# Feed-forward products of a decoder trunk: from wide and narrow matmuls in turn to runs of one width

## Chip, core and metric

The kernel runs on one core of a Trainium2 chip. The metric is the device time of one execution in microseconds (us). The time before is the median of three runs.

## What is computed

Two decoder layers work on 256 tokens of width 1024. Each layer is a half-step feed-forward block, a mixer, and a second half-step feed-forward block. Layer 0 mixes with a convolution beside attention over a memory, layer 1 with block attention beside attention over the memory; a shared key and value projection stands between the layers. The change touches the four feed-forward blocks alone.

```python
def swiglu(x, w_gate, w_up, w_down):          # 1024 -> 2816, twice, and 2816 -> 1024
    return (jax.nn.silu(x @ w_gate) * (x @ w_up)) @ w_down

for layer in range(2):
    ...
    h = h + 0.5 * swiglu(rms_norm(h, ffn1_norm_g[layer]), ...)
    hn = rms_norm(h, mix_norm_g[layer])
    ...                                        # the mixer, and its output projection
    h = h + 0.5 * swiglu(rms_norm(h, ffn2_norm_g[layer]), ...)
```

## The kernel before, in words

Activations lie transposed: a tile has 128 features on the partitions and the 256 tokens along a row. Weights stream from HBM in chunks of 128x2048 floats (tile `raw`, three buffers, issued by the queue of SP). Each chunk is two halves of 128x1024, and a half holds eight weight tiles of 128x128.

Products are made to nearly full float precision from two parts of each operand. ScalarE (ACT) rounds a half to its high part (tile `wh`, line 180), and VectorE (DVE) subtracts to get the low part (tile `wl`, line 184). Both have four buffers, so the halves are converted ahead of their use. The activations `y` lie as a high and a low part side by side, 256 columns each. A weight tile then needs two matmuls on TensorE (PE): a *wide* one, high weights by both parts of the activation, 512 columns into `o`; and a *narrow* one, low weights by the high part, 256 columns into the first half of `o`. `mm2` issues this pair, wide and then narrow, for each weight tile; every matmul has another stationary operand. `both_halves` adds the two halves of `o` later (ACT copies one, DVE adds).

`ffn` is called four times, with names a (the first), b, c and d. For each of the 22 tiles `j` of the hidden width it makes the gate product (`pg`, eight weight tiles over `k`, tiles named `ag`, `bg`, `cg`, `dg`) and the up product (`pu`, named `au` and so on), and from them the hidden tile `hs`. Then for each of eight output tiles `m` it makes the down product (`po`, named `ao` and so on) over 22 weight tiles. For `m` below 7 these are pairs by `mm2`; for `m = 7` they are three narrow matmuls each by `mm3`. So an `ffn` has 2 x 176 + 154 = 506 pairs and 66 narrow matmuls.

Two starts differ. In block a (`first`), the four products of `j = 0, 1` share the first weight halves, since these come in late. In the other blocks, at `j = 0`, the last of the eight `k` stands behind the other seven of both products, because its activation is ready last.

Inside `ffn` a scheduler orders each engine's queue by its own model of time (`state["order"]` is empty there), so instructions of neighbouring groups can be interleaved; in other parts the order is fixed by `in_order`. PSUM tiles for gate, up and down products come from four buffers in turn. In block a the function `prepare` is hooked in at `j = 5` (position angles, sines, and statistics of the memory on DVE, ACT and POOL) and at `j = 9`.

Of the kernel before, what the change touches and what calls it, by code (L numbers as in the profile page):

```python
# [19 lines left out]
KD = DM // P  # L20
SEQ = 256
NT = SEQ // P
DFF = 2816
KF = DFF // P
# [59 lines left out]
def tile_kernel(ctx: ExitStack, tc: tile.TileContext, w, xT, memT, pos, vec, hg, const, out):  # L84
# [39 lines left out]
    nc.vector.memset(mhalf, -0.5)  # L124


    state = {"chunk": 0, "half": 0, "raw": None, "order": "", "last": {}}

    def behind(i, other):
        tc.add_manual_dep(i.ins, other.ins.name,  # L130
                          mybir.DependencyInfo(mybir.DependencyClass.NoSync, mybir.DependencyReason.DATA),
                          reason="issue order")

    def in_order(engine, i):

        last = state["last"].get(engine)
        if engine in state["order"] and last is not None:
            behind(i, last)
        state["last"][engine] = i
        return i  # L140

    def tables(func):

        behind(nc.scalar.activation(warm, onec, func), state["func"])

    def mmul(*a, **k):
        return in_order("P", nc.tensor.matmul(*a, **k))  # L147
# [40 lines left out]
    def half_chunk():  # L188
        wh, wl, parts, hi, lo = half_hi()
        for s in parts:  # L190
            hi(s)
            lo(s)
        return wh, wl

    def tiles_of(n_half):
        for n in range(n_half):
            wh, wl = half_chunk()
            for i in range(8):
                yield wh[:, i * P:(i + 1) * P], wl[:, i * P:(i + 1) * P]

    def mm3(o, wt, y, k, first, last, **kw):
        h, l = wt
        i = mmul(o, h, y[:, k, 0], start=first, stop=False, **kw)
        mmul(o, h, y[:, k, 1], start=False, stop=False, **kw)
        mmul(o, l, y[:, k, 0], start=False, stop=last, **kw)
        return i

    def mm2(o, wt, y, k, first, last):

        h, l = wt  # L210
        mmul(o, h, y[:, k].rearrange("p a s -> p (a s)"), start=first, stop=False)
        mmul(o[:, :SEQ], l, y[:, k, 0], start=False, stop=last)

    def mm_group(o, y):
        for k, wt in enumerate(tiles_of(1)):
            mm3(o[:, :SEQ], wt, y, k, k == 0, k == KD - 1)

    def mm_group2(o, y):
        for k, wt in enumerate(tiles_of(1)):
            mm2(o, wt, y, k, k == 0, k == KD - 1)  # L220

    def both_halves(name, o, tag):

        c = tp.tile([P, SEQ], F32, name=name + "c", tag="cvq")
        nc.scalar.activation(c, o[:, SEQ:], AF.Copy)
        a = tp.tile([P, SEQ], F32, name=name, tag=tag)
        nc.vector.tensor_tensor(a, o[:, :SEQ], c, op=ALU.add)  # L227
        return a
# [7 lines left out]
    def psum(name, tag="mm", bufs=4):  # L236
        return ps.tile([P, 512], F32, name=name, tag=tag, bufs=bufs)
# [29 lines left out]
    def square_sum(name, acc, src, first, adder=nc.gpsimd):  # L267
        if first:
            nc.scalar.activation(acc, src, AF.Square)
        else:  # L270
            sq = tp.tile([P, SEQ], F32, name=name, tag="sq")
            nc.scalar.activation(sq, src, AF.Square)
            adder.tensor_tensor(acc, acc, sq, op=ALU.add)
# [32 lines left out]
    def norm_stats(name, acc):  # L306
        r = rstd_cols(name + "r", acc)
        return r, bcast_rows(name + "b", r)

    def new_acc(name):  # L310
        return tp.tile([P, SEQ], F32, name=name, tag="acc")

    def ffn(name, y, acc, nexts, store=False, both=False, hook=None, after=None, hook_down=None):

        hs = cp.tile([P, KF, 2, SEQ], F32R, name=name + "hs", tag="hs")
        rb, first = None, acc is None
        for j in range(KF):
            if hook and j > 1:
                with tc.issue_after(state["act"].ins), tc.issue_after(state["dve"].ins), \
                        tc.issue_after(state["sync"].ins):  # L320
                    hook(j)
            if first and j == 0:

                four = [psum(f"{name}{'gu'[i % 2]}{i // 2}") for i in range(4)]
                it = tiles_of(4)
                for k in range(KD):
                    for o in four:
                        mm2(o, next(it), y, k, k == 0, k == KD - 1)
                acc = new_acc(name + "acc0")
                nc.scalar.dma_start(cst, const)  # L330

                sq = cp.tile([P, KD, SEQ], F32, name="sq0", tag="kv")
                for k in range(KD):
                    nc.scalar.activation(sq[:, k], x[:, k], AF.Square)
                n = KD
                while n > 1:
                    n //= 2
                    add = nc.vector.tensor_tensor(acc if n == 1 else sq[:, :n].rearrange("p k s -> p (k s)"),
                                                  sq[:, :n].rearrange("p k s -> p (k s)"),
                                                  sq[:, n:2 * n].rearrange("p k s -> p (k s)"), op=ALU.add)  # L340
                    if n == KD // 2:
                        behind(add, state["dve"])
            if first and j < 2:
                pg, pu = four[2 * j:2 * j + 2]
            else:

                at = ("sc", 2) if first and j == 2 else ()
                pg, pu = psum(f"{name}g{j}", *at), psum(f"{name}u{j}", *at)
                if j == 0:

                    wts = [list(tiles_of(1)) for _ in range(2)]
                    for ks in (range(KD - 1), (KD - 1,)):
                        for o, wt in zip((pg, pu), wts):
                            for k in ks:
                                mm2(o, wt[k], y, k, k == 0, k == KD - 1)
                else:
                    mm_group2(pg, y)
                    mm_group2(pu, y)
            if rb is None:
                _, rb = norm_stats(name + "n", acc)  # L360
            g = both_halves(f"{name}gs{j}", pg, "g")
            nc.vector.tensor_tensor(g, g, rb, op=ALU.mult)
            s = tp.tile([P, SEQ], F32, name=f"{name}s{j}", tag="s")
            state["func"] = nc.scalar.activation(s, g, AF.Silu)
            h = both_halves(f"{name}h{j}", pu, "h")
            nc.vector.tensor_tensor(h, h, s, op=ALU.mult)
            nc.scalar.activation(hs[:, j, 0], h, AF.Copy)
            nc.vector.tensor_tensor(hs[:, j, 1], h, hs[:, j, 0].bitcast(F32), op=ALU.subtract)
        if after:
            tables(after)  # L370
        ys = [(y_both if both else y_tiles)(f"{name}y{i}") for i in range(len(nexts))]
        acc = new_acc(name + "acc")
        it = tiles_of(KD * KF // 8)
        for m in range(KD):
            po = psum(f"{name}o{m}")
            if hook_down:
                with tc.issue_after(state["act"].ins):
                    hook_down(m)

            both_sums = m < KD - 1  # L380
            for k in range(KF):
                if both_sums:
                    mm2(po, next(it), hs, k, k == 0, k == KF - 1)
                else:
                    mm3(po[:, :SEQ], next(it), hs, k, k == 0, k == KF - 1)
            if both_sums:
                d = both_halves(f"{name}d{m}", po, "g")
                nc.vector.scalar_tensor_tensor(d, d, 0.5, rb, op0=ALU.mult, op1=ALU.mult)
            else:
                d = tp.tile([P, SEQ], F32, name=f"{name}d{m}", tag="g")  # L390
                nc.vector.scalar_tensor_tensor(d, po[:, :SEQ], 0.5, rb, op0=ALU.mult, op1=ALU.mult)
            nc.vector.tensor_tensor(x[:, m], d, x[:, m], op=ALU.add)
            if store:
                nc.sync.dma_start(out[m], x[:, m])
                continue
            last = both and m == KD - 1
            if last:
                square_sum(f"{name}q{m}", acc, x[:, m], False, nc.vector)
            for yy, g in zip(ys, nexts):
                scaled_split(yy, x[:, m], m, g, last)  # L400
            if not last:
                square_sum(f"{name}q{m}", acc, x[:, m], m == 0)
        return ys, acc
# [264 lines left out]
    y = y_tiles("y0")  # L668
# [176 lines left out]
    last = psum("cvp2")  # L845
# [44 lines left out]
    for c in range(CC):  # L890
# [4 lines left out]
        for i in range(NT):  # L895
            mmul(pv[:, i * P:(i + 1) * P], sq[:, i * P:(i + 1) * P], onem, start=c == 0 and i == 0, stop=c == CC - 1,
                 skip_group_check=True)
# [64 lines left out]
    for k, (wh, wl, *_) in enumerate(halves):  # L962
        for m in range(KD):
            s = slice(m * P, (m + 1) * P)
# [6 lines left out]
    it = tiles_of(CC - FIRST_CAT)  # L971
# [4 lines left out]
    y = ys  # L976
# [49 lines left out]
    y, acc = next(oproj)  # L1026
# [127 lines left out]
```

## Time and profile before

| | |
|---|---|
| median of three runs | 999.71 us (997.63 to 999.74) |
| span of the profiled execution | 994.6 us |
| PE busy | 980.1 us, 5788 matmuls |
| DVE busy | 734.1 us |
| ACT busy | 593.8 us |
| HBM read, written | 171.43 MB, 1.05 MB: 173 GB/s over the span |

The profile shows one execution from the first to the last instruction, and lists no time of its own outside that span; the median of the runs lies 5.1 us above the span. A matmul's record lasts longer than its share of PE: the records of neighbours overlap, so what a matmul costs is read from start to start, or from a stretch divided by its count. The chain of waits merges neighbours of one tile and gives start, length and count. The PE clock is granted in full in all 40 slices.

### The profile page before, as it was taken

The numbers are of one execution on the slowest core, as the hardware profiler recorded it, in microseconds if no ns is written. First come the engines' busy times: TensorE is split into PE (matmuls) and PEld (weight loads), VectorE is DVE, ScalarE is ACT, GpSimd is POOL, SyncE is SP. The second block draws the span as 40 slices with busy tenths as digits, with TensorE's granted clock in tenths as the row PEclk, the third lists the DMA queues.
The fourth block names the chain that finished last, engine by engine and source line by source line (L and its number), as shares of the span: only waits on it lengthen the run. The fifth ranks groups of instructions, "written<-read, shape, count | busy, mean of one in ns | idle before, by whom it ended". The sixth has DMA issues, their size and how long they took to land.

```text
span 994.6 us, 15556 instructions
## 1 busy us (share of the span) xinstructions
PE 980.1 (99%) x5788; PEld 850.3 (85%) x5788; DVE 734.1 (74%) x1326; ACT 593.8 (60%) x1154; POOL 129.1 (13%) x151
## 2 busy tenths in 40 slices
PE   9899999999999999999999999999998999999998
PEld 7788888898779888888888888888995898888887
DVE  7987776679966877777776777767788587777663
ACT  6675577747576655555646555555556656555542
POOL 0301000138712000000123000000142030000000
PEclk9999999999999999999999999999999999999999
DMA  9555555533325555545555545555442055455560
GB/s 329 205 206 172 206 173 187 195 128 128 127 94 203 193 189 175 206 170 195 186 175 206 170 170 195 187 178 203 172 172 82 25 193 207 171 194 186 175 227 22
DMA packets 26427, 173.47 MB, mean 174 GB/s; under 512 B 3184, under 2 KB 4848, under 8 KB 6000
## 3 DMA queue, kind: packets, MB, share of 16 engines
q1 hardware_dynamic: 26064, 172.31, 49.3%
q8 instruction: 45, 0.74, 0.3%
q14 instruction: 30, 0.25, 0.1%
q10 hardware_dynamic: 288, 0.17, 0.1%
HBM read 171.43 MB, written 1.05 MB: 173 GB/s over the span
## 4 chain that ended last, share of the span: by engine, by line
PE 90%; ACT 3%; DVE 3%; POOL 2%; DMA 1%; issue 1%; POOLq 0%; ACTq 0%; DVEq 0%
PE cg L147 7%; PE dg L147 6%; PE bg L147 6%; PE du L147 6%; PE bu L147 6%; PE do L147 6%; PE co L147 6%; PE bo L147 6%; PE ao L147 6%; PE cu L147 6%; PE ag L147 5%; PE au L147 5%; PE kv L147 3%; PE oao L147 2%; PE obo L147 2%; PE mkv L147 2%
## 5 line engine op out<-in xcount | busy, mean ns | idle before, releaser
L184 DVE TENSOR_TENSOR wl<-raw,wh 128x1024 fp32r<-128x1024 f32 (+1 forms) x310 | 377.2, 1219 | 179.7 <-ACT wh L180 179.2
L180 ACT ACTIVATE wh<-raw 128x1024 fp32r<-128x1024 f32 (+1 forms) x310 | 324.1, 1048 | 306.2 <-PE dg L147 28.4
L147 PE MATMUL ag<-y,wh 128*128 128x512 f32 x176 | 63.9, 398 | 2.0 <-DVE ags L227 1.6
L147 PE MATMUL cg<-by,wh 128*128 128x512 f32 x176 | 63.3, 399 | 0.8 <-DVE cgs L227 0.8
L147 PE MATMUL dg<-oby,wh 128*128 128x512 f32 x176 | 63.6, 400 | 0.0
L147 PE MATMUL bg<-oay,wh 128*128 128x512 f32 x176 | 63.6, 399 | 0.0
L147 PE MATMUL bu<-oay,wh 128*128 128x512 f32 x176 | 63.4, 398 | 0.0
L147 PE MATMUL cu<-by,wh 128*128 128x512 f32 x176 | 63.4, 399 | 0.0
L147 PE MATMUL du<-oby,wh 128*128 128x512 f32 x176 | 63.4, 399 | 0.0
L147 PE MATMUL au<-y,wh 128*128 128x512 f32 x176 | 63.3, 394 | 0.0
L147 PE MATMUL do<-dhs,wh 128*128 128x512 f32 (+1 forms) x198 | 61.9, 369 | 0.0
L147 PE MATMUL co<-chs,wh 128*128 128x512 f32 (+1 forms) x198 | 61.9, 369 | 0.0
L147 PE MATMUL bo<-bhs,wh 128*128 128x512 f32 (+1 forms) x198 | 61.9, 369 | 0.0
L147 PE MATMUL ao<-ahs,wh 128*128 128x512 f32 (+1 forms) x198 | 61.9, 369 | 0.0
L147 PE MATMUL cu<-by,wl 128*128 128x256 f32 x176 | 49.6, 282 | 0.0
L147 PE MATMUL co<-chs,wl 128*128 128x256 f32 x176 | 49.6, 283 | 0.0
L147 PE MATMUL ao<-ahs,wl 128*128 128x256 f32 x176 | 49.6, 283 | 0.0
L147 PE MATMUL do<-dhs,wl 128*128 128x256 f32 x176 | 49.6, 283 | 0.0
L147 PE MATMUL bo<-bhs,wl 128*128 128x256 f32 x176 | 49.6, 283 | 0.0
L147 PE MATMUL cg<-by,wl 128*128 128x256 f32 x176 | 49.4, 281 | 0.0
L147 PE MATMUL du<-oby,wl 128*128 128x256 f32 x176 | 49.4, 281 | 0.0
L147 PE MATMUL dg<-oby,wl 128*128 128x256 f32 x176 | 49.4, 281 | 0.0
(996 smaller groups left out, 2436.0 us busy)
## 6 DMA issues: line engine op xcount, KB each, us to landing
raw<-in_w SPq DMA_DIRECT2D x158, 1024.0 KB, 4.8
raw<-in_w SPq DMA_DIRECT2D x5, 512.0 KB, 8.1
mT<-in_memT SPq DMA_DIRECT2D x1, 1024.0 KB, 8.3
out<-x SPq DMA_DIRECT2D x8, 128.0 KB, 1.7
raw<-in_w SPq DMA_DIRECT2D x2, 256.0 KB, 3.9
x<-in_xT SPq DMA_DIRECT2D x1, 512.0 KB, 6.9
x<-in_xT SPq DMA_DIRECT2D x2, 128.0 KB, 3.3
x<-in_xT SPq DMA_DIRECT2D x1, 256.0 KB, 4.4
```

Source lines behind the costliest of these rows:

```text
L147: return in_order("P", nc.tensor.matmul(*a, **k))
L180: state["act"] = nc.scalar.activation(wh[:, s], raw[:, s], AF.Copy)
L184: state["dve"] = nc.vector.tensor_tensor(wl[:, s], raw[:, s], wh[:, s].bitcast(F32), op=ALU.subtract)
```

## The change

A group of eight weight tiles is no longer issued as eight pairs. All eight matmuls of one width are issued, then all eight of the other. Groups take turns (`next_turn`): the first has its high parts first, the next its low parts first, so that the end of one group and the start of the next have the same width. In the down products the groups follow the eight tiles of a weight half across the borders of `m` (`lead`, `cuts`). At the start of block a the four products issue four wide, then four narrow; at `j = 0` of the other blocks the runs have seven, and the last `k` is apart. The number of matmuls, their operands and the weight loads stay as they are.

```diff
-    def mm2(o, wt, y, k, first, last):
-        h, l = wt
-        mmul(o, h, y[:, k].rearrange("p a s -> p (a s)"), start=first, stop=False)
-        mmul(o[:, :SEQ], l, y[:, k, 0], start=False, stop=last)
+    def mm_run(jobs, y, low_first=False):
+        passes = []
+        for o, wt, k in jobs:
+            passes.append((o, wt[0], y[:, k].rearrange("p a s -> p (a s)")))
+        for o, wt, k in jobs:
+            passes.append((o[:, :SEQ], wt[1], y[:, k, 0]))
+        return passes[len(jobs):] + passes[:len(jobs)] if low_first else passes
+
+    def mm_passes(passes, first=True, last=True):
+        for i, (o, w_, y_) in enumerate(passes):
+            mmul(o, w_, y_, start=first and i == 0, stop=last and i == len(passes) - 1, skip_group_check=True)
+
+    def next_turn():
+        state["flip"] = not state["flip"]
+        return not state["flip"]
...
     def mm_group2(o, y):
-        for k, wt in enumerate(tiles_of(1)):
-            mm2(o, wt, y, k, k == 0, k == KD - 1)
+        mm_passes(mm_run([(o, wt, k) for k, wt in enumerate(tiles_of(1))], y, next_turn()))
...
-                        for o, wt in zip((pg, pu), wts):
-                            for k in ks:
-                                mm2(o, wt[k], y, k, k == 0, k == KD - 1)
+                        runs = [mm_run([(o, wt[k], k) for k in ks], y, i == 1)
+                                for i, (o, wt) in enumerate(zip((pg, pu), wts))]
+                        for run in runs:
+                            mm_passes(run, ks[0] == 0, ks[0] > 0)
...
-            for k in range(KF):
-                if both_sums:
-                    mm2(po, next(it), hs, k, k == 0, k == KF - 1)
-                else:
+            if both_sums:
+                lead = -m * KF % 8
+                cuts = [0] * (lead > 0) + list(range(lead, KF, 8)) + [KF]
+                for a, b in zip(cuts, cuts[1:]):
+                    jobs = [(po, next(it), k) for k in range(a, b)]
+                    mm_passes(mm_run(jobs, hs, next_turn()), a == 0, b == KF)
+            else:
+                for k in range(KF):
                     mm3(po[:, :SEQ], next(it), hs, k, k == 0, k == KF - 1)
```

In block d, gate and up products on PE, one `j` and the start of the next (`wh` is the high, `wl` the low weight tile; 128x512 is a wide matmul, 128x256 a narrow one). Before:

```order
L147 MATMUL dg_8703<-oby,wh_0_8707 128x512
L147 MATMUL dg_8703<-oby,wl_0_8708 128x256
...
L147 MATMUL du_8704<-oby,wh_1_8727 128x512
L147 MATMUL du_8704<-oby,wl_1_8728 128x256
...
L147 MATMUL dg_8761<-oby,wh_0_8765 128x512
L147 MATMUL dg_8761<-oby,wl_0_8766 128x256
```

and now, where `x8` stands for eight in a row:

```order
L147 MATMUL dg_8703<-oby,wl_0_8708 128x256 x8
L147 MATMUL dg_8703<-oby,wh_0_8707 128x512 x8
L147 MATMUL du_8704<-oby,wh_1_8727 128x512 x8
L147 MATMUL du_8704<-oby,wl_1_8728 128x256 x8
L147 MATMUL dg_8761<-oby,wl_0_8766 128x256 x8
L147 MATMUL dg_8761<-oby,wh_0_8765 128x512 x8
```

The width changed at every matmul; now it changes after sixteen, eight of gate and eight of up.

In the down products of block b, at the border from the output tile `bo_4755` to `bo_4827`, PE issued the pairs of a weight half one after another:

```order
L147 MATMUL bo_4755<-bhs,wh_1_4802 128x512
L147 MATMUL bo_4755<-bhs,wl_1_4803 128x256
...
L147 MATMUL bo_4827<-bhs,wh_1_4802 128x512
L147 MATMUL bo_4827<-bhs,wl_1_4803 128x256
...
L147 MATMUL bo_4827<-bhs,wh_0_4838 128x512
L147 MATMUL bo_4827<-bhs,wl_0_4839 128x256
```

and now the half is cut at the border, and both cuts are runs:

```order
L147 MATMUL bo_4755<-bhs,wl_1_4803 128x256 x4
L147 MATMUL bo_4755<-bhs,wh_1_4802 128x512 x4
L147 MATMUL bo_4827<-bhs,wh_1_4802 128x512 x4
L147 MATMUL bo_4827<-bhs,wl_1_4803 128x256 x4
L147 MATMUL bo_4827<-bhs,wl_0_4839 128x256 x8
L147 MATMUL bo_4827<-bhs,wh_0_4838 128x512 x8
```

Most runs of the down products have eight to sixteen matmuls.

The scheduler also moved work on DVE. At the start of block a (`kk`, `rr` are steps of the angles; `anb` the row of the norm, `anbp` its source in PSUM; `ags_389<-ag_343` and `ah_396<-au_344` empty the PSUM buffers of the products of `j = 3`), DVE had before:

```order
L692 CAST posf<-pt 128x2
L695 TENSOR_SCALAR ang<-cst,posf 128x8 x2
...
L303 COPY anb<-anbp 128x256
...
L227 TENSOR_TENSOR ags_389<-ag_343,ags3c 128x256
...
L184 TENSOR_TENSOR wl_1_608<-raw_585,wh_1_607 128x1024
L362 TENSOR_TENSOR ags_389<-ags_389,anb 128x256
L227 TENSOR_TENSOR ah_396<-au_344,ah3c 128x256
```

and now:

```order
L710 CAST posf<-pt 128x2
L313 COPY anb<-anbp 128x256
L713 TENSOR_SCALAR ang<-cst,posf 128x8 x2
...
L237 TENSOR_TENSOR ags_389<-ag_343,ags3c 128x256
...
L291 TENSOR_SCALAR rm_v<-rm_p 128x2
L184 TENSOR_TENSOR wl_1_608<-raw_585,wh_1_607 128x1024
L237 TENSOR_TENSOR ah_396<-au_344,ah3c 128x256
```

The copy of `anb` moved ahead of the angles, and the emptying of `au_344` came to stand further behind that of `ag_343`.

More of the change, by code (lines that the diff above doesn't have):

```diff
@@ L124, in tile_kernel @@
     nc.vector.memset(mhalf, -0.5)
-    state = {"chunk": 0, "half": 0, "raw": None, "order": "", "last": {}}
+    state = {"flip": False, "chunk": 0, "half": 0, "raw": None, "order": "", "last": {}}
     def behind(i, other):
@@ L326, in ffn @@
                 for k in range(KD):
-                    for o in four:
-                        mm2(o, next(it), y, k, k == 0, k == KD - 1)
+                    wts = [next(it) for _ in four]
+                    for o, wt in zip(four, wts):
+                        mm_passes(mm_run([(o, wt, k)], y)[:1], k == 0, False)
+                    for o, wt in zip(four, wts):
+                        mm_passes(mm_run([(o, wt, k)], y)[1:], False, k == KD - 1)
                 acc = new_acc(name + "acc0")
```

## The prediction

> **What bounds the kernel now.** I read first the page's busy times and the shares of the chain that ended last.
>
> ```profile
> PE 980.1 (99%) x5788; PEld 850.3 (85%) x5788; DVE 734.1 (74%) x1326; ACT 593.8 (60%) x1154; POOL 129.1 (13%) x151
> PE 90%; ACT 3%; DVE 3%; POOL 2%; DMA 1%; issue 1%; POOLq 0%; ACTq 0%; DVEq 0%
> ```
>
> PE carries the kernel from end to end, with as many matmuls after the change as before. What counts is the step from one matmul's start to the next. So I read next the chain of waits in order of time (start, length, engine, tile, count), for the price of a pair of one wide and one narrow matmul.
>
> ```profile
> 84.94 2.79 PE ag L147 x16
> 145.97 61.88 PE ao L147 x374
> 302.48 10.43 PE oao L147 x87
> 331.53 2.82 PE bg L147 x16
> 438.94 61.88 PE bo L147 x374
> 818.90 2.83 PE du L147 x16
> 849.99 2.83 PE dg L147 x16
> 861.30 2.83 PE dg L147 x16
> 929.14 61.90 PE do L147 x374
> ```
>
> Between the first `bg` row and `bo` lie 38 groups of eight pairs: (438.94 - 331.53)/304 = 353.3 ns a pair. Block d gives (929.14 - 818.90)/312 = 353.3 over 39 groups. Block a, with the same instructions, gives (145.97 - 84.94)/176 = 346.8 over 22. So the same pair has two prices, and nothing in the work tells them apart. The timeline of PE shows how the dear one is made up (start, duration, tile):
>
> ```profile
> 837.10 0.40 PE L147 MATMUL du<-oby,wh 128*128 128x512 f32 x1
> 837.34 0.28 PE L147 MATMUL du<-oby,wl 128*128 128x256 f32 x1
> 837.46 0.40 PE L147 MATMUL du<-oby,wh 128*128 128x512 f32 x1
> 837.70 0.28 PE L147 MATMUL du<-oby,wl 128*128 128x256 f32 x1
> 837.81 0.40 PE L147 MATMUL du<-oby,wh 128*128 128x512 f32 x1
> 838.04 0.28 PE L147 MATMUL du<-oby,wl 128*128 128x256 f32 x1
> 838.16 0.40 PE L147 MATMUL du<-oby,wh 128*128 128x512 f32 x1
> ```
>
> Three pairs take 1.06 us: wide steps of 0.24, 0.24, 0.23 (mean 0.237), narrow ones of 0.12, 0.11, 0.12 (mean 0.117). Now the places of the same kernel where matmuls of one width already stand together, from the same timeline: the start of block a (four wide, four narrow, twice), the memory's keys and values (all wide), and the last output tile of block b (66 narrow, up to the first `kv`).
>
> ```profile
> 14.66 0.40 PE L147 MATMUL ag<-y,wh 128*128 128x512 f32 x1
> ...
> 15.59 0.28 PE L147 MATMUL ag<-y,wl 128*128 128x256 f32 x1
> ...
> 17.47 0.40 PE L147 MATMUL ag<-y,wh 128*128 128x512 f32 x1
> ...
> 62.19 0.39 PE L147 MATMUL mkv<-wh,my 128*128 128x512 f32 x1
> ...
> 65.86 0.62 PE L147 MATMUL mkv<-wh,my 128*128 128x512 f32 x2
> ...
> 492.83 0.39 PE L147 MATMUL bo<-bhs,wh 128*128 128x256 f32 x2
> ...
> 500.65 0.39 PE L147 MATMUL kv<-wh,by 128*128 128x512 f32 x1
> ```
>
> In fours a wide step is 0.93/4 = 232.5 ns, and the two rounds, 14.66 to 17.47, cost 2.81/8 = 351.3 ns a pair. The first sixteen wide steps after alternating ones, 62.19 to 65.86, average 3.67/16 = 229.4. The 66 narrow steps average 7.82/66 = 118.5, and the 87 of the `oao` row above 10.43/87 = 119.9.
>
> **The change, part by part.** It adds and removes no matmul, weight load, conversion or DMA. It changes a matmul's neighbours, and by that the step.
>
> *Gate and up of b, c and d.* Runs of sixteen. I take 229.4 for a wide step and 119.2, the middle of 118.5 and 119.9, for a narrow one: 348.6 ns a pair, 4.7 less than 353.3 (block c is put at the price of b and d). Over 3 x 352 = 1056 pairs that is -5.0 us. The lower end is a wide run that has settled:
>
> ```profile
> 62.35 10.92 PE mkv L147 x48
> ```
>
> (227.5 ns in the whole run; with 118.5 that is 346.0 a pair, -7.7 us.) The upper end is the price in fours, 351.3: -2.1 us. I take the row whose run has the length of the new ones.
>
> *Down products.* Of the 374 matmuls of a row, 66 are narrow ones in a run (7.8 us), so a pair now costs (61.88 - 7.82)/154 = 351.0 ns. The new runs have mostly eight to sixteen, between the fours at 351.3 and the sixteens at 348.6; I take 349.5. Over 4 x 154 = 616 pairs: -0.9 us, from -3.1 (at 346.0) to +0.2 (at 351.3).
>
> *Gate and up of a.* Here the pair is already at 346.8, and sixteens would be dearer. The 22 groups above are 176 pairs: +1.8 ns each is +0.3 us, from -0.1 (at 346.0) to +0.8 (at 351.3).
>
> *The conversions.* A low-first run needs all of `wl` at its start, and a high-first run holds it to its end. ACT and DVE are far ahead (the bracket: idle time before, and who ended it):
>
> ```profile
> 852.74 1.06 ACT L180 ACTIVATE wh<-raw 128x1024 fp32r<-128x1024 f32 x1 [1.20 <-PE dg L147]
> 853.83 1.23 DVE L184 TENSOR_TENSOR wl<-raw,wh 128x1024 fp32r<-128x1024 f32 x1 [0.74 <-ACT wh L180]
> ```
>
> ACT stands idle until PE has finished the group of 849.99 and given back its `wh`; with four buffers this tile serves the group of 861.30. Its `wl` is done at 855.06, 6.2 us ahead. A run gives back one of its two buffers sooner than now and the other at the group's end, as now; so the cover stays, SP's loads wait for no one new, and the part costs nothing. Were the cover gone, a group would wait for one `wl`, 1.23 us.
>
> *Where PE waits for DVE.* PE stands still at the start of block a and in block c, until DVE has emptied a PSUM buffer. The rows: DVE and PE in a, and the page's group for c (its last numbers are the idle time and who ended it).
>
> ```profile
> 39.37 0.41 DVE L227 TENSOR_TENSOR ags<-ag,ags3c 128x256 f32<-128x256 f32 x1
> 41.91 0.41 DVE L227 TENSOR_TENSOR ah<-au,ah3c 128x256 f32<-128x256 f32 x1
> 42.94 2.77 PE au L147 x16
> L147 PE MATMUL cg<-by,wh 128*128 128x512 f32 x176 | 63.3, 399 | 0.8 <-DVE cgs L227 0.8
> ```
>
> In DVE's new order the copy of `anb` stands ahead of the angles and one `wl` fewer ahead of `ags_389<-ag_343`. I put this row some 1.3 us sooner (one `wl` of 1.23 and some small steps, less 0.4 for another `ah`), at 38.1 to 38.5. But between it and `ah_396<-au_344`, which frees the buffer for the next `au` group, there are now two `wl` (1.2 each), four more steps of 0.4 and some small ones: about 4.5 us, so 42.6 to 43.0. The `au` group starts at 42.94 now. What is won at the first buffer is late again at the second, and PE's own gain before that point is swallowed with it: 0, from -1.5 to +1. In block c the transposes of the norm row stand behind more narrow and fewer wide matmuls, some 0.5 us sooner: -0.4 us of the 0.8, from -0.8 to +0.5.
>
> *The starts of b and d.* There the runs of seven take `y` in another order, and the last tile of `y`, whose low part DVE makes last, is wanted a little sooner after the projection. In d:
>
> ```profile
> 808.19 0.96 DVE L264 SCALAR_TENSOR_TENSOR oby<-x,vt,oby 128x256 fp32r<-128x256 f32 x1
> 811.40 0.47 PE L147 MATMUL dg<-oby,wh 128*128 128x512 f32 x1
> ```
>
> It is done at 809.15 and first used at 811.40. By the new order 19 wide and 21 narrow matmuls stand ahead of that last `k`, about 6.9 us at the steps above against some 7.5 now. A margin of 1.6 us is left: 0, from 0 to +1.
>
> *The sum.* -5.0 - 0.9 + 0.3 + 0 - 0.4 + 0 = -6.0 us on the span of 994.6, so 988.6. The median of the runs stands 5.1 us above that span, which the change doesn't touch: 999.7 - 6.0 = 993.7 us. All lower ends together would be -13.2, all upper ones +1.4.
>
> **A rule that speaks against it.** The rows give a step that depends on the neighbours: 346.8, 351.3 and 353.3 ns for the same pair. The Trainium skill, page "TensorE: Matmul & The Clock Gate", section "Wait — 56ns, not 53.3ns?", has a step of N / 2.4 GHz and a fixed 2.5 ns at full clock. By it a pair costs 325 ns in any order, so the change would be worth nothing. The trace disagrees in the size and, more to the point, in that the extra is not fixed.
>
> **The rivals.**
>
> *Order is no matter.* If the two prices come from something other than the alternation (a phase that PE falls into at the start of a stretch and keeps), the runs would fall into one as well, and the mean price would stay: 999.7 us. For it speaks that block a alternates at 346.8 all the same, and that fours, a kind of run, cost 351.3. Against it: in every wide run above the step is below the 0.237 of the alternation, by more than the narrow ones give back. With all three products at 351.3 the terms are -2.1 + 0.2 + 0.8 - 0.4 = -1.5, or 998.2; so this case covers 998 to 1001.
>
> *Runs settle at once.* Wide 227.5 and narrow 118.5 from the first matmul on, the lower ends: -7.7 - 3.1 - 0.1 - 0.4 = -11.3, or 988.4 us. Against it stands that the sixteen of `mkv` at 62.19 begin dearer than they end (229.4 to 227.5).
>
> *Runs are dearer: slower.* If a change of width throws PE out of step and a run of sixteen never comes back, its wide matmuls stay at the 0.237 of the alternation, while the narrow ones lose their 0.117 and take 119.2: 355.9 ns a pair. That is +2.6 x 1056 + 4.9 x 616 + 9.1 x 176 = +7.4 us, with -0.4 from block c +7.0, or 1006.7. The mean pair of these three parts is now 351.9; above that the kernel is slower, below it faster. No wide run in the trace reaches 0.237, not even the fours, so I give it little.
>
> **How the numbers follow.** A measurement of this kernel tells about 0.2%, 2 us, from no change. The forecast (a pair in sixteens between 347.5 and 350.5 ns; 991 to 997.5) gets 0.60. Settled at once gets 0.15. Order is no matter, 0.17, of which a quarter comes out faster by more than 2 us. Dearer runs get 0.08. Faster: 0.60 + 0.15 + 0.04 = 0.79; same 0.13; slower 0.08. The range from 987.5 to 999 leaves out the slower case and part of the third, some 0.18; the forecast's own range is 991 to 997.5.
>
> **What would show it.** In the chain of waits a pair of groups (16 wide, 16 narrow) in b, c and d takes 5.58 us where two groups take 5.65 now, if the price is right; in block a 5.58 where it is 5.55. The down rows fall from 61.9 to about 61.6 us. The timeline should show the first wide steps of a run near 0.232 and the last near 0.227. The `au` group of `j = 5` should start within a microsecond of 42.9. I am wrong if groups in b and d stay at 2.82, if PE waits for `wl` at the head of low-first groups, or if idle time shows up at the starts of b and d.

## Result, and the profile after

The changed kernel takes 988.89 us (median of 4 executions, 988.57 to 990.57), beside 999.15 us for the kernel before on the same chip (4 executions, 997.63 to 999.74). The ratio is 0.9901, with a 95% interval of 0.9887 to 0.9914. The forecast was 993.7 us; 988.89 lies inside the range given (987.5 to 999) and outside the forecast's own (991 to 997.5).

The page's busy times and the shares of the chain that ended last, and two groups: the conversions on DVE, and the gate products of block c, where PE waited for DVE (the last numbers are idle time and its releaser):

```profile
PE 974.9 (99%) x5788; PEld 850.7 (86%) x5788; DVE 744.0 (75%) x1326; ACT 601.4 (61%) x1154; POOL 134.0 (14%) x151
PE 90%; ACT 3%; DVE 3%; POOL 2%; DMA 1%; issue 1%; SPq 0%; POOLq 0%; ACTq 0%; DVEq 0%
L184 DVE TENSOR_TENSOR wl<-raw,wh 128x1024 fp32r<-128x1024 f32 (+1 forms) x310 | 377.1, 1220 | 103.0 <-ACT wh L180 98.9
L147 PE MATMUL cg<-by,wh 128*128 128x512 f32 x176 | 43.9, 391 | 0.3 <-DVE cgs L237 0.3
```

PE is still the chain and has as many matmuls as before. DVE's conversions still wait for ACT; the idle time in block c went from 0.8 to 0.3 us.

The chain of waits in order of time (start, length, engine, tile, count):

```profile
83.35 2.80 PE ag L147 x16
144.62 61.91 PE ao L147 x374
330.24 2.80 PE bg L147 x16
333.04 2.77 PE bu L147 x16
436.01 61.94 PE bo L147 x374
815.95 2.80 PE dg L147 x16
921.71 61.94 PE do L147 x374
```

From the `bg` row of 330.24 to `bo` there are 38 groups: (436.01 - 330.24)/304 = 347.9 ns a pair. Block d gives (921.71 - 815.95)/304 = 347.9, and block a (144.62 - 83.35)/176 = 348.1, where it had 346.8. The down rows did not fall (61.88 to 61.90 before). The timeline of PE in block d shows one change of width and back:

```profile
837.10 1.11 PE L147 MATMUL du<-oby,wl 128*128 128x256 f32 x8
838.05 1.12 PE L147 MATMUL dg<-oby,wl 128*128 128x256 f32 x8
839.01 2.00 PE L147 MATMUL dg<-oby,wh 128*128 128x512 f32 x8
840.85 1.98 PE L147 MATMUL du<-oby,wh 128*128 128x512 f32 x8
842.66 1.11 PE L147 MATMUL du<-oby,wl 128*128 128x256 f32 x8
```

Eight wide steps behind narrow ones take 840.85 - 839.01 = 1.84 us, 230 ns each; the next eight 1.81 us, 226 ns each. A run starts dear and settles. By the starts in the trace, in ns, the first five wide steps are 234, 236, 228, 232 and 231 and the rest 227; the first narrow step is 113 and the rest 119 to 120. That is 26 ns lost and some 7 won, 19 ns for one change of width and back.

The span fell by 7.4 us, from 994.6 to 987.2. By place, from the starts of the rows: up to the down products of a -1.35, of which 0.35 is no work of the change (the first load landed sooner, and the first matmul began at 12.80 us in place of 13.15); gate and up of b 113.06 to 111.32 and of d the same, -1.74 each; of c 126.47 to 124.32, with its stall, -2.15; the mixer of layer 1 -0.7; the four down products +0.2. But the medians differ by 10.3 us. The experiments had to explain both: why the pair costs 347.9, and where 3 us come from that the two traces don't show.

### The profile page after: what moved, and what is told of

It reads as the page before. It is cut to its first block, busy times and chain, and to the rows that moved or that the text cites. A ratio compares the mean times of both kernels' runs of the same rounds, so it can differ in the third digit from the quotient of the medians.

```text
span 987.2 us, 15410 instructions
## 1 busy us (share of the span) xinstructions
PE 974.9 (99%) x5788; PEld 850.7 (86%) x5788; DVE 744.0 (75%) x1326; ACT 601.4 (61%) x1154; POOL 134.0 (14%) x151
## 4 chain that ended last, share of the span: by engine, by line
PE 90%; ACT 3%; DVE 3%; POOL 2%; DMA 1%; issue 1%; SPq 0%; POOLq 0%; ACTq 0%; DVEq 0%
PE cg L147 7%; PE co L147 6%; PE do L147 6%; PE bo L147 6%; PE ao L147 6%; PE dg L147 6%; PE bg L147 6%; PE bu L147 6%; PE du L147 6%; PE cu L147 6%; PE au L147 5%; PE ag L147 5%; PE kv L147 3%; PE oao L147 2%; PE obo L147 2%; PE mkv L147 2%
## 5 line engine op out<-in xcount | busy, mean ns | idle before, releaser
L833 POOL TENSOR_TENSOR hc<-hc,cq 128x256 f32<-128x256 f32 x58 | 42.6, 737 | 12.5 <-ACT cq L832 8.7
L147 PE MATMUL cg<-by,wh 128*128 128x512 f32 x176 | 43.9, 391 | 0.3 <-DVE cgs L237 0.3
L147 PE MATMUL du<-oby,wh 128*128 128x512 f32 x176 | 44.0, 389 | 0.0
L841 DVE SCALAR_TENSOR_TENSOR cvp<-hc,vt,cvp 128x256 f32<-128x256 f32 x88 | 40.6, 485 | 1.5
L147 PEld LDWEIGHTS ao<-ahs,wh 128*128 128x128 f32 x198 | 34.9, 188 | 5.8
L147 PEld LDWEIGHTS co<-chs,wh 128*128 128x128 f32 x198 | 34.8, 188 | 5.7
L147 PEld LDWEIGHTS do<-dhs,wh 128*128 128x128 f32 x198 | 34.8, 188 | 5.7
L147 PEld LDWEIGHTS bo<-bhs,wh 128*128 128x128 f32 x198 | 34.8, 188 | 5.7
L147 PEld LDWEIGHTS ag<-y,wh 128*128 128x128 f32 x176 | 33.1, 189 | 7.3 <-ACT wh L180 0.6
L147 PEld LDWEIGHTS cg<-by,wh 128*128 128x128 f32 x176 | 32.9, 188 | 7.5 <-DVE cgs L237 0.7
```

The costliest lines, as they stand in the source:

```text
L833: state["pool"] = nc.gpsimd.tensor_tensor(cv[:, c], cv[:, c], q, op=ALU.add)
L841: nc.vector.scalar_tensor_tensor(cv[:, c] if end else o, win(c, i), tap[c][i], o, op0=ALU.mult, op1=ALU.add)
```

## The experiments

Theory after the comparison: a pair settles at some 346.7 ns (the price in block a before), and each change of width and back costs a fixed 20 ns or less, shared by the run. Rival: PE falls into a phase in each stretch, and the order is no matter. A second question was the place of the gain (products, start of block a, something outside the span).

**Gate and up alone.**

```diff
-                    jobs = [(po, next(it), k) for k in range(a, b)]
-                    mm_passes(mm_run(jobs, hs, next_turn()), a == 0, b == KF)
+                    for k in range(a, b):
+                        mm_passes(mm_run([(po, next(it), k)], hs), k == 0, k == KF - 1)
```

> Runs of one width in the gate and up products alone; the down products go back to wide and narrow in turn. Theory (runs pay in gate and up, and nothing in down): nearly the whole gain is kept, the ratio to before is 0.989 to 0.992, a run of 16 wide and 16 narrow takes 5.57 us in b, c and d, and the down rows stay at 61.9 us. The prediction's own sizes say that 0.9 us of the gain go away. A rival, that the down products gain outside what one profile shows: 2 to 3 us less gain, a ratio of 0.993 or above.

Measured: 991.48 us against 999.88, ratio 0.9916 (0.9901 to 0.9932).

**Down products alone** (gate, up and the start of block a go back to pairs in the same way).

> Runs in the down products alone; gate and up go back to pairs. Theory: nothing is gained, the ratio is 0.998 to 1.001, the down rows are at 61.9 us, a group of eight pairs takes 2.82 us in b, c and d. The prediction's size: -0.9 us, 0.999. If the start of block a gains about 1 us only because of what the scheduler moves, it gains nothing here where its order is as before.

Measured: 999.50 us, ratio 1.000 (0.999 to 1.0011). The chain of this kernel:

```profile
334.01 2.82 PE bg L147 x16
931.67 61.94 PE do L147 x374
```

Runs are worth nothing in the down products: 61.94 with them, 61.88 to 61.90 as pairs in the kernel before. The whole gain is in gate and up, or in what comes with them.

**No turns.** High parts first in each group, so runs of eight.

```diff
     def next_turn():
-        state["flip"] = not state["flip"]
-        return not state["flip"]
+        return False
```

> High parts first in every group, so that the width changes after 8 matmuls and not after 16. Theory (each return to wide matmuls costs a fixed time, 17.5 ns or so in sum, and the pair settles at 346.7 ns): a pair costs 346.7 + 17.5/8 = 348.9 ns in place of 347.9, over 1232 pairs of gate and up 1.3 us more than with turns; ratio to before 0.991 to 0.993, a group of eight 2.79 us. Rival (a phase that PE falls into, whatever the order): the time is that of the changed kernel, 0.990, or the pair jumps to 353 in single blocks.

Measured: 992.93 us, ratio 0.9933 (0.9917 to 0.9948), just above what was expected. From the chain, 39 groups of block b:

```profile
331.09 2.79 PE bu L147 x16
440.03 1.17 PE bo L147 x5
```

(440.03 - 331.09)/312 = 349.2 ns a pair, where 348.9 was expected. The blocks agree with one another, so no phase decides here. The time is some 3 us above that of the changed kernel by the ratios, more than the 1.3 us of the pairs; the start of block a also has another order, with waits of 0.62 and 1.57 us and, over 40 to 44 us, a mean clock of 0.57.

**The kernel before, once more, with a profile of its own.**

> The kernel before, once more, with a profile of its own. Theory: the profiled execution of before was one of its faster ones. All runs here have 1.7 us outside the span, so the median of before belongs to a span near 997.5, 3 us above the 994.6 of the profile shown, and the difference lies in block a, whose pair then costs 353 ns and not 346.8 (+1.1 us over its 22 groups) or at its start. Rival: the span is 994.6 again with 5 us outside it, and block a stays at 346.8.

Measured: 998.96 us (996.21 to 1000.86), the profiled execution 998.81 with a span of 997.0. Only 1.8 us lie outside its span. In the executions timed after it this difference is 1.7 to 1.9 us, and 75 executions of the kernel before in four sessions have spans with a median of 998.0. The profiled execution of before, 994.6, was one of the shortest. The cause was not the one I expected. Block a again ran at 346.8. A table by stretch shows the first part of it (busy time of each engine, then the granted clock, DMA share and GB/s), first of the profile known before:

```profile
core 0: us, PE busy (x) PEld busy (x) DVE busy (x) ACT busy (x) POOL busy (x), PEclk, DMA share, GB/s
40.00:44.00 4.00, 4.00 (x23) 3.55 (x24) 3.77 (x12) 2.50 (x6) 0.71 (x1) 1.00 0.34 84
```

and of this one:

```profile
40.00:44.00 4.00, 3.56 (x13) 3.11 (x14) 4.00 (x12) 1.55 (x4) 0.71 (x1) 0.57 0.33 74
```

Right behind the waits in block a (1.09 and 1.65 us in both) the clock was granted at half for about 3.4 us (a mean of 0.57 over 4 us: 0.43 x 4, twice). The timeline of PE shows what that does to a pair:

```profile
41.00 0.41 PE L147 MATMUL ag<-y,wl 128*128 128x256 f32 x1
41.22 0.63 PE L147 MATMUL ag<-y,wh 128*128 128x512 f32 x1
41.64 0.41 PE L147 MATMUL ag<-y,wl 128*128 128x256 f32 x1
```

A pair takes 0.64 us there, not 0.35. From the gate group behind those waits to the down products it is 1.4 us longer than in the first profile. The second part lies in the mixer of layer 1. The same table there, two rows of the first profile and then two of this one:

```profile
753.00:760.00 7.00, 5.75 (x34) 3.63 (x35) 6.93 (x30) 3.34 (x14) 1.23 (x2) 0.76 0.36 139
763.00:767.00 4.00, 4.00 (x34) 2.22 (x33) 2.66 (x11) 1.85 (x7) 0.00 (x0) 1.00 0.02 4
753.00:760.00 7.00, 6.24 (x27) 3.38 (x28) 6.73 (x29) 2.82 (x12) 1.23 (x2) 0.53 0.36 140
763.00:767.00 4.00, 3.67 (x16) 2.06 (x18) 1.34 (x5) 0.55 (x3) 0.00 (x0) 0.58 0.00 0
```

The mixer takes 2.5 us longer here. So the first profile was not at full clock either: it has some 3.4 us at half in this place (0.24 x 7, twice). Ten of the thirteen traces without added matmuls in the mixer, that of the changed kernel among them, have a stretch at half there. The page's row of 40 slices hides all this: a slice of 25 us with 3.4 us at half still shows a 9, which I had read as full.

In block c this execution does something else. The chain, right after the stall and at the block's end:

```profile
561.30 3.04 PE cg L147 x16
567.12 2.77 PE cg L147 x16
655.87 2.77 PE cg L147 x16
```

The same code as in the first profile, but 2.77 us a group where that had 2.83; block c wins 1.9 us by it. The span of this execution is 2.4 us longer in sum: 0.5 from a later first load, 1.4 in block a and 2.5 in the mixer, less the 1.9. So alternating matmuls have two prices with nothing in the code between them. Start to start, in ns, the dear pattern repeats after three pairs, 236+113, 233+117, 241+120. The cheap one is 230+117 all along in block a; in block c of this execution 231+113 and 232+118 take turns, at the same mean. In blocks a and c of both profiles the change from dear to cheap comes at two transposes that stand between a wide and a narrow matmul.

**A knock.** The kernel before, with two transposes added, once in each of b, c and d, whose result is not used.

```diff
+            if k == knock:
+                pk = psum("kn", "aux", 2)
+                state["order"] = "P"
+                for i in range(2):
+                    transp(pk[:, i * P:(i + 1) * P], ident, ident)
...
-                    mm_group2(pg, y)
+                    mm_group2(pg, y, {("b", 3): 3, ("c", 6): 4, ("d", 3): 3}.get((name, j)))
```

> The kernel before, wide and narrow in turn, with two transposes of the identity (the result is not used) put between a wide matmul and its narrow one, once in each of the blocks b, c and d (at j = 3, 6 and 3, each behind a wide step of 236 ns). Theory of two patterns: the alternation runs in one of two locked patterns, 236+113, 233+117, 241+120 ns (353.3 a pair) or 230+117 (346.7), and an interruption of this kind moves it from the dear to the cheap one, as the transposes of block a did at 81.6 us and those of block c at 545 us. Then the groups behind the two transposes take 2.77 us in place of 2.83, 854 pairs x 6.6 ns less 3 x 0.22 us: -5.0 us, a ratio of 0.994 to 0.997 to before. Rival (each change of width has a price of its own, so only runs help): groups stay at 2.82 to 2.83, the ratio is 0.999 to 1.002.

Measured: 996.06 us against 1000.09, ratio 0.996 (0.9944 to 0.9976). The chain in block b:

```profile
335.54 1.30 PE bg L147 x7
336.83 0.22 PE kn L150 x2
338.57 2.77 PE bu L147 x16
441.19 61.98 PE bo L147 x374
```

Behind the two transposes the rest of the block runs at (441.19 - 338.57)/296 = 346.7 ns, and so do c and d behind theirs. Six instructions that do nothing useful give back 4 us. The 353.3 of before was not the price of a change of width. It was that of one pattern, the one that b and d fell into in every trace in which they alternate.

**Runs of 32.** Gate and up of one `j` together.

```diff
-                    mm_group2(pg, y)
-                    mm_group2(pu, y)
+                    wts = [list(tiles_of(1)) for _ in range(2)]
+                    both_o = [mm_run([(o, wt, k) for k, wt in enumerate(ws)], y) for o, ws in zip((pg, pu), wts)]
+                    order = (1, 0) if next_turn() else (0, 1)
+                    for n_, half in enumerate(order):
+                        for r in both_o:
+                            mm_passes(r[half * KD:(half + 1) * KD], n_ == 0, n_ == 1)
```

> The changed kernel with the gate and up products of one j taken together, so that the width changes after 32 matmuls. Theory (346.7 ns a pair and 17.5 ns for each change of width and back): 347.2 a pair in place of 347.9, 1232 pairs x 0.6 = -0.7 us against the changed kernel, a ratio of 0.989 to 0.990; a gate and up product of one j take 5.555 us. Rival (two halves of weights are now held to the end, and the conversions come too late): PE waits for wl or wh, and the time is 1 us or more above that of the changed kernel.

Measured: 998.97 us, ratio 0.9987 (0.9977 to 0.9998). The theory had the pair right and the rival the loss, though not its reason. The chain in block b, and the timeline of PE in block a:

```profile
404.63 0.96 PE bg L147 x8
437.97 0.96 PE bg L147 x8
```

```profile
43.55 2.04 PE L147 MATMUL ag<-y,wl 128*128 128x256 f32 x8 [4.68 <-DVE rm_v L291]
```

Six `j` take 33.34 us, 347.3 ns a pair. PE waits for no conversion; but DVE's order at the start of a leaves it idle for 4.68 us, and some 7 us at half the clock follow: some ten times what the longer runs win.

**hs 128 bytes further on.** In the down products a wide run never settled (in the changed kernel the sixteen wide steps from 445.21 us average 232 ns and end as dear as they began), and their moving operand is `hs`. Three small tiles are put ahead of it; the 128 bytes are reckoned from their sizes, as no trace shows an address.

```diff
+        if acc is None:
+            small.append(cp.tile([P, NT], F32, name="posf"))
+            small.append(cp.tile([P, NT, HALF], F32, name="ang"))
+            cp.tile([P, NT], F32, name="qe0", tag="qe")
         hs = cp.tile([P, KF, 2, SEQ], F32R, name=name + "hs", tag="hs")
```

> The changed kernel with the tile hs, the moving operand of the down products, 128 bytes further on in SBUF (three small tiles are put ahead of it; other large operands stay where they are). Theory (a run of wide matmuls settles at 227 ns only where weights and moving operand have the same address modulo 256 bytes, as y and cat have, and hs has not): the down rows fall from 61.9 us to (154 x 347.9 + 66 x 119.9 ns) 61.5 us or below, a median 1 to 2 us under that of the changed kernel, a ratio of 0.988 to 0.989. Rival: the address is no matter, down rows at 61.9, the ratio of the changed kernel (0.990).

Measured: 989.96 us against 1000.09, ratio 0.9898 (0.9881 to 0.9915). The chain:

```profile
436.46 61.53 PE bo L148 x374
920.46 61.54 PE do L148 x374
```

All four down rows fell by 0.4 us, to (61.54 - 7.82)/154 = 348.8 ns a pair, and a run of sixteen wide steps now settles at 227. So the place of the moving operand in SBUF sets whether such a run settles; smaller tiles behind it move as well, but gate and up, which don't use `hs`, keep their step. That it is the address modulo 256 relative to the weights' is not shown: moving all tiles together was not tried. The 1.6 us don't show in the median, and the ratio is that of the rival, since the spans of its five executions go from 985.5 us at a mean clock of 1.0 to 990.0 at 0.995.

**Block a alone, and b, c, d alone.** Runs in gate and up of one part, the rest as before.

```diff
-                    mm_group2(pg, y)
+                    mm_group2(pg, y, first)        # the other kernel: not first
```

> Runs of one width in the gate and up products of block a alone; all the rest as before. Runs are no cheaper there (348.1 ns a pair against 346.7, +0.3 us), so what is gained comes from the new order at the start of the block. Theory (the gain beyond the products: PE waits 1.76 us once, and no longer 1.1 and 1.65 us in a row, and so it also keeps its clock, where before loses some 1.5 us to half the clock): -1 us of waiting and -1.5 us of clock, a median 1.5 to 3.5 us lower, ratio 0.9965 to 0.9985, the slices 40 to 44 us at full clock. Rival (the prediction: nothing is won at the start of a): 1.000 to 1.001.

> Runs of one width in the gate and up products of blocks b, c and d alone; block a and the down products as before. Theory: 353.3 to 348.1 ns over 1056 pairs, -5.5 us, and -0.7 us in the mixer of layer 1: a ratio of 0.9935 to 0.9955, with PE waiting 1.1 and 1.65 us in block a and the half clock behind it in most executions, as before. Rival (the whole gain lies in the products of b, c and d): 0.990 to 0.992.

Measured in one session: a alone 995.85 us, ratio 0.9961 (0.9948 to 0.9973); b, c, d alone 994.57, ratio 0.9957 (0.9942 to 0.9972). Together that is 0.8% and agrees with gate and up in one kernel (0.9916). Each lies just outside its expectation, a alone as the larger gain, b, c and d as the smaller. Almost half of the gain comes with block a, where the pair even got dearer. Table by stretch and timeline of PE for a alone:

```profile
40.00:44.00 4.00, 4.00 (x16) 3.43 (x15) 4.00 (x12) 3.00 (x6) 1.62 (x1) 0.57 0.60 240
```

```profile
39.22 0.60 PE L147 MATMUL rm_p<-onec,macc 128*128 128x1 f32 x4 [1.75 <-POOL macc L287]
```

With the new order PE waits once, 1.75 us, and not for 1.09 and 1.65. At full clock, in the changed kernel, the way from the first matmul to the down products is 1.0 us shorter by it (131.8 us where before has 132.8). I had expected the half clock to be gone, and in this execution it is not. In the kernel with gate and up alone the same wait had full clock behind it:

```profile
40.00:44.00 4.00, 4.00 (x26) 3.61 (x25) 4.00 (x12) 3.28 (x7) 1.62 (x1) 1.00 0.66 250
```

So after one wait of 1.75 us it is chance: of the four traces with it, two have the half clock right behind it. After the two waits of before it is nearly the rule: of five traces with these, four have it. For the other executions only the mean clock is known, not the place. One stretch of 3.4 us at half takes 0.0017 from the mean. Of the 75 executions of before only 6 have 0.998, about one such stretch, and none has 1.0; of the 12 of a alone three have 1.0. The span mostly goes with the mean clock: it averages 995.2 us in those 6, 996.8 in the 11 at 0.996, 998.6 in the 37 at 0.995. But the 9 at 0.993 average 997.9, so the clock is not all; the pattern of block c is worth 1.9 us.

**Matmuls to keep PE busy.** First in the kernel before, in the wait of block a alone.

```diff
+            if first and j == 5:
+                state["order"] = "P"
+                pf = psum("fill", "sc", 2)
+                for i in range(6):
+                    mmul(pf, busy[:, :P], busy, start=True, stop=True)
```

> The kernel before with six matmuls on constants (the result is not used) at the head of the j = 5 gate product of block a, where PE waits 1.65 us for DVE. Theory (the 2.7 us of idle time around 36.6 to 39.9 us cost before, in most executions, some 3.4 us at half the clock right after): the granted clock stays at 1.0 between 40 and 44 us in each execution, the mean clock is 0.996 to 0.998 in place of 0.995, and the median is 1.0 to 2.0 us lower, a ratio of 0.998 to 0.999. Rival (the clock falls there for another reason): the same time as before, the slice 40 to 44 us at half the clock in most executions.

Measured: 999.07 us against 1000.09, ratio 0.9993 (0.998 to 1.0005). Not conclusive. The clock was full where the matmuls were added, and in this execution it fell in two other places. The first of them, and block a:

```profile
12.00:16.00 4.00, 4.00 (x16) 3.37 (x15) 4.00 (x10) 3.89 (x10) 0.00 (x0) 0.57 0.96 389
42.00:46.00 4.00, 3.66 (x21) 3.01 (x20) 4.00 (x13) 2.19 (x7) 0.72 (x1) 1.00 0.39 100
```

The half clock came at 12 us, behind a wait of 2.48 us for the first weight tiles, and again in the mixer of layer 1, with a mean of 0.57 over 766 to 770 us.

**Both gains together.** `hs` moved, and runs of 32 in b, c and d (the edits as above).

> The changed kernel with the tile hs 128 bytes further on, and with the gate and up products of b, c and d in runs of 32 (block a keeps its runs of 16, and so its order). Theory: the down rows stay at 61.4 us in place of 61.8 (-1.6 us against the changed kernel), a gate and up product of one j takes 5.555 us in place of 5.57 (1056 pairs x 0.6 ns, -0.6 us), no waits in block a beyond the 0.4 and 1.4 us that the kernel with hs moved has: span 985 to 986 at full clock, ratio 0.986 to 0.9885. Rival (the starts of the blocks give it back): 0.989 to 0.991.

Measured: 994.06 us against 999.47, ratio 0.9951 (0.9934 to 0.9968): the rival, and worse. From the timeline of PE in block c:

```profile
560.03 3.75 PE L148 MATMUL cg<-by,wh 128*128 128x512 f32 x8 [3.17 <-ACT chs L394]
```

The stall of block c grew to 3.17 us, and 7 us at half the clock followed (a mean of 0.58 over 558 to 566 us). This execution also has half the clock in block a (0.57 over 40 to 44 us) and in the mixer of layer 1.

**hs moved, and PE kept busy in three waits.**

```diff
+    def fill(n, dst):
+        state["order"] += "P"
+        for i in range(n):
+            mmul(dst, busy[:, :P], busy, start=True, stop=True)
...
+                    if k == 1:
+                        fill(4, pw)
...
+        fill(5, psum("fill", "sc", 2))
         nc.vector.tensor_copy(rm, rstd_cols("rm_", macc))
...
+        if name == "am10":
+            fill(5, pp[0])
```

> The changed kernel with hs moved by 128 bytes, and with matmuls on constants (results not used) where PE stands idle for a microsecond or more: four where it waits for the third weight tile at the start of block a, five ahead of the memory's statistics (rm_p), five ahead of the first transposes of attention in the mixer of layer 1. Theory (what is left of the spread between executions is half the clock for 3.4 us behind such idle times): the mean clock is 0.998 to 1.0 in nearly all executions, no slice of the trace but the last at half the clock, the span near 985 us, a median 1 to 3 us below that of the kernel with hs moved, ratio 0.9865 to 0.989, with a smaller spread. Rival (the extra matmuls take what they save, or the clock falls all the same): 0.9895 to 0.991.

Measured: 987.61 us against 1000.40, ratio 0.9874 (0.985 to 0.9897), and all five executions between 987.41 and 987.75. The span and mean clock, and the added matmuls with the wait left behind them, from the timeline of PE:

```profile
core 0: 985.6 us, clock 1.000
```

```profile
9.79 1.04 PE L148 MATMUL pw<-busy 128*128 128x512 bf16 x4
36.84 1.25 PE L148 MATMUL fill<-busy 128*128 128x512 bf16 x5
39.12 2.09 PE L148 MATMUL ag<-y,wh 128*128 128x512 f32 x8 [0.69 <-DVE ags L243]
746.93 1.24 PE L148 MATMUL am10pp<-busy 128*128 128x512 bf16 x5
```

All five executions have a mean clock of 1.000, where one of the five with `hs` moved alone had it, and the distance between the fastest and the slowest falls from 4.5 us to 0.3. The added matmuls are not the only difference: in block a PE waited 0.40 and 1.41 us in the kernel with `hs` moved, and here 0.69 us once. This version is faster than the kernel before, and its slowest execution is below the fastest of the changed kernel (988.57), though these ran in two sessions and the intervals of the ratios overlap.

## Why the prediction was right, and where it was not

**Gate and up of b, c, d: right.** -5.0 us at 348.6 ns a pair; the traces give 347.9, which would be (353.3 - 347.9) x 1056 = -5.7 us. Read by block it is 1.74 + 1.74 + 2.15, less 0.5 for c's stall, -5.1 us, and the kernel with b, c and d alone gained 4.3 us by its ratio (2.8 to 5.8). The wide steps go from 230 to 226 ns where I had put 232 and 227. The reason was half right. The runs do leave the dear alternation, but that was one pattern of the alternation and not its price, and the rival "order is no matter" had its mechanism: PE falls into a phase at the start of a stretch and keeps it. I gave it 0.17 and assumed that runs would fall into one as well. They don't: 347.3, 347.9 and 349.2 ns in runs of 32, 16 and 8, with 346.7 as what all approach, which is also the cheap alternation. By these, a change of width and back costs about 20 ns, and the steps of a run in the trace after give 19.

**Down products: mis-sized.** The step "between the fours at 351.3 and the sixteens at 348.6" took the price of gate and up for another moving operand. Predicted -0.9 us, measured none: (61.94 - 7.82)/154 = 351.4 ns a pair, with 351.0 before. With `hs` moved it is 348.8.

**Gate and up of a: right.** +1.3 ns a pair, +0.2 us, where +0.3 was put.

**Conversions, starts of b and d, stall of c: right.** No gate or up group of b or d shows idle time in the page, and c's stall fell by 0.5 us, predicted 0.4.

**Start of block a: the step failed.** I said that what is won at the first buffer is lost at the second, because the `au` group of `j = 5` waits for `ah_396<-au_344`. The timeline of PE and DVE after:

```profile
37.85 0.61 PE L147 MATMUL rm_p<-onec,macc 128*128 128x1 f32 x4 [1.77 <-POOL macc L283]
41.22 1.12 PE L147 MATMUL au<-y,wl 128*128 128x256 f32 x8
41.79 0.41 DVE L237 TENSOR_TENSOR ah<-au,ah3c 128x256 f32<-128x256 f32 x1
```

The group began at 41.22, and that emptying at 41.79: it used a buffer that was free already (`ags` of `j = 4` was done at 40.58). "Four buffers in turn" was wrong: this group took what was free. PE waits for POOL once, and the start of the block gains 1.0 us in place of 0; `au` was to start within a microsecond of 42.9 and did so 1.7 us sooner.

**"5.1 us above that span, which the change doesn't touch": failed.** Only 1.75 us lie outside the span. The rest was that the profiled execution was a lucky one, mostly in its clock: spans of before have a median of 998.0. The change seems to touch just that. With one wait in place of two in block a, three of the four executions after have a mean clock of 0.998; that the wait did it is argued from the traces of block a and not shown by itself. The Trainium skill, page "TensorE: Matmul & The Clock Gate", section "What's actually happening", has the clock set by a free-running window of 3.4 us, at half after an idle one. The 3.4 us and the element of chance agree with these runs (a mean clock of 0.57 over 4 us in one profile of before, and 1.00 in the other). Its table in "Why this matters for your kernels" lets idle times of up to about 3 us pass; here 1.75 us were enough, with four one-column matmuls behind them.

**The mixer of layer 1** I had not looked at. The wait for `q1T` is shorter, first before and then after:

```profile
762.43 1.19 PE L147 MATMUL ab2s<-kvs,q1T 64*128 64x128 f32 x8 [1.75 <-ACT q1T L433]
```

```profile
756.80 1.19 PE L147 MATMUL ab2s<-kvs,q1T 64*128 64x128 f32 x8 [0.95 <-ACT q1T L451]
```

The code there is the same; the scheduler made another order. The clock does not tell the two apart: its mean over 750 to 760 us is 0.83 in both profiles. The kernel with block a alone has the 0.95 too, and that with b, c, d alone the 1.75, so it comes with the edit in block a; how, was not followed. So block a alone gains 3.6 us by the medians: 1.0 at its start, 0.8 here, and a rest that fits half clocks avoided but was not measured by itself.

So the total, -10.3 us by the medians, is -5.1 in the products of b, c and d, -2.3 in waits, the first load and the down products, and some 3 us by which the profiled execution of before was better than its median, mostly in the clock. The forecast had the first and left out nearly all of the others. That 988.89 lies inside the range is luck in part: the range reaches so low for the "settled" rival at 988.4, whose own mechanism (346.0 a pair, down products too) did not happen.

## What to carry to other kernels

Read matmul prices from start to start over whole stretches, and when one instruction mix shows two prices, look for a pattern that locks before crediting an order: a second profile of the same kernel is the cheapest test. Look at the granted clock in stretches of a few microseconds behind each wait of over a microsecond; with a few matmuls on constants in such waits, nearly all of the spread was gone here. Before a profile's span is set against a median, ask for the spans of the other executions.

## What the runs showed of the hardware that I had not expected

- Alternating matmuls of 512 and 256 columns lock into patterns of two prices, 353.3 or 346.7 ns a pair; two 128-column transposes between a wide and a narrow one moved b, c and d from the first to the second.
- A change of width and back costs a stream of such matmuls some 20 ns, over the first five wide steps.
- Moving the moving operand of the down products by the reckoned 128 bytes took their pair from 351.4 to 348.8 ns.
- Waits of 1.09 and 1.65 us in a row were followed by 3.4 us at half the clock in one profile of the kernel before and not in the other; 1.4 us of time went with it in block a. A single wait of 1.75 us was followed by it in two of four traces.
